# First projection weight tile and first two modulation tiles loaded whole, and every operation placed anew, in one layer of a hybrid RG-LRU and sparse-attention block

## The chip, the cores and the metric

The kernel runs on one core of one Trainium2 chip. The time is the device time of one execution in microseconds (us); lower is better. A profile shows one execution, with its own time. Engines are named as the profile names them: PE (matrix products; PEld is its loading of the stationary operand), DVE, ACT, POOL, and SP, which here only issues transfers. A few transfers are issued by ACT.

## The reference

One layer over 512 tokens of width 1024, batch 1, all in float32. What the opening of the kernel computes is the modulation and the normalised, modulated input:

```
mod = jax.nn.silu(c) @ ada_w[l] + ada_b[l]
sh1, sc1, g1, sh2, sc2, g2 = jnp.split(mod, 6, axis=-1)
h = modulate(rms_norm(x, pre_norm_mix[l]), sh1, sc1)      # h * (1 + sc1) + sh1
y = hybrid_mixer(h, w_in[l], ...)                         # z = h @ w_in, two head groups, @ w_out
x = x + (1.0 + g1) * rms_norm(y, post_norm_mix[l])
h = modulate(rms_norm(x, pre_norm_mlp[l]), sh2, sc2)
y = jnp.square(jax.nn.relu(h @ w_ff1[l])) @ w_ff2[l]
x = x + (1.0 + g2) * rms_norm(y, post_norm_mlp[l])
```

The mixer projects h, feeds one half of the columns to a gated linear recurrence with a causal convolution, and the others to an attention of three branches (compressed, selected and windowed keys), normalises both halves and projects them back. The last part is an MLP of width 4096 with a squared ReLU.

## The kernel before, in words

Float32 products are made of three float32r products: each operand is split into a rounded part (`hi`) and the rest (`lo`), and hi*hi, hi*lo and lo*hi are summed in PSUM. So for each weight tile an engine writes `hi` from the raw tile, another writes `lo = raw - hi`, and PE then has three products for each block.

**Opening.** Four x tiles of 128 x 1024 (`r_1` and `r_2` in the profile, two in each) are loaded by SP; each is normalised with a sum of squares (written to `att` as waste) and a power on POOL. The conditioning vector comes in two small transfers issued by ACT: `in_ccol` (128 x 8), of which `sil` is computed, and `in_vecs` (128 x 136), the gains and biases. From `sil` and the identity matrix `ident`, PE makes `silb`, silu(c) in a row, the same in every partition: four products for each half of it (`tp_104`, `tp_105`), which an engine then copies out. `ident`, `tab` and `ctab` (the last two are masks for the attention) are made on DVE.

**The wave.** The first projection takes 768 columns of h in eight steps j, one for each 128 input features. For each j two modulation tiles (`p`, 128 x 1024, from `in_ada_a`) are multiplied by `silb` and summed along the row on DVE (`ada_sums`): that gives 128 shifts and 128 scales, `sa`. PE transposes the four x blocks into `tp`; ACT writes h = tp * scale + shift, once rounded (`h_136`, `h_137`, ... are j = 0, 1, ...) and once exact (`pt`); DVE writes the rest (`h_144`, `h_145`, ...). Weight tile `raw_a` is split into `hi_a` and `lo_a`. Then come 18 products of 512 columns for each j: six PSUM tiles (two each of `f`, `s`, `pv`) by three products. Names of j = 0: tiles p_158 (shift) and p_159 (scale), sa_166, raw_a_160. Of j = 1: p_161, p_162, sa_176, raw_a_163. Of j = 2: p_164, p_165, sa_184.

Before the first product, 18 products of ones with ones (`s<-ones`) run on PE; nothing reads their result.

**What sets the order.** Each operation is recorded (`Clocks.put`, `flush`) and then issued in an order written out by hand: `PLAN` is a string of two characters for each operation, which are its place among all of them. `PLACE` is a string for each part of the program with one letter for each operation that more than one engine can do: a (ACT), d (DVE) or p (POOL). On each engine the instructions run in that order; semaphores keep the dependences. SP's and ACT's transfers are places in the same order. A place number says nothing about a time: an operation waits until its engine has reached it and its inputs are there.

In j = 0 the kernel loads the first two `p` tiles in halves of 512 columns and sums each half by itself, the second sum starting from the first one's result; and it loads `raw_a_160` in three pieces of 256 columns. All other tiles are loaded whole. `hi_a` and `lo_a` of j = 0 are made in pieces of 256 columns.

**After the wave.** The rest of the projections, the recurrence, the attention (scores `s`, probabilities `p`, transposed `pt`, weighted values `pv`), the output projection, and the MLP follow, in which blocks of products are merged to save some of them (`first_pair`, `up_pair`). PE has work of this kind until shortly before the end, and the output rows are normalised and stored.

Of the kernel before, what the change touches and what calls it, by code (L numbers as in the profile page):

```python
# [11 lines left out]
ALU = mybir.AluOpType  # L12
PSUM = bass.MemoryType.PSUM

P = 128
S = 512
# [1918 lines left out]
```

## Time and profile before

| | |
|---|---|
| median of 3 runs | 588.01 us |
| lowest and highest | 586.90, 588.99 us |
| the profiled execution's own time | 588.5 us |
| its span, first to last instruction | 586.7 us |
| PE, DVE, ACT, POOL busy | 572.7 (98%), 550.1 (94%), 416.5 (71%), 227.2 (39%) us |
| transfers | 89.12 MB, 192 issued by SP |

The execution that was profiled took 1.8 us more than its span, and 0.5 us more than the median of the runs. In a row of the timeline the first two numbers are the start and the length in us, `x16` counts merged instructions, and the bracket has the idle time of the engine before it and what ended that. A product in float32 shows two instructions for each one in the program's order.

### The profile page before, as it was taken

Reading aid. Unit: us, or ns where it says so; the run is one execution under the profiler, and the core shown is the slowest. Engines: PE = TensorE matmul, PEld = TensorE weight load, DVE = VectorE, ACT = ScalarE, POOL = GpSimd, SP = SyncE. Lnnn points to the kernel's source line nnn. Section 1 sums busy time; section 2 is a strip of 40 time slices with the busy share of each in tenths; the row PEclk is TensorE's granted clock in tenths of the full one; section 3 lists DMA queues with packets and bytes.
Section 4 is the critical chain, followed back from the end, with each engine's and each line's share of the span. In section 5 each row is a group of like instructions: output and inputs, shape, how many; then the busy total and the mean of one; then the engine's idle time right before and its main releaser. Section 6 shows DMA issues by size and latency. Waiting matters only on the chain.

```text
span 586.7 us, 9981 instructions
## 1 busy us (share of the span) xinstructions
PE 572.7 (98%) x3410; PEld 499.5 (85%) x3410; DVE 550.1 (94%) x1143; ACT 416.5 (71%) x849; POOL 227.2 (39%) x212
## 2 busy tenths in 40 slices
PE   6999999999999999999999999999999999999995
PEld 5688889878888898899999999998778888788884
DVE  5999999999999999999999999999999999998877
ACT  6658877999999999788747666574757676555314
POOL 4203323656847288651234242532101400114453
PEclk9999999999999999999999999999999999999999
DMA  8989895142242410022342423337343444344303
GB/s 314 417 314 344 295 396 220 59 142 73 94 177 91 151 65 1 19 91 73 109 147 106 139 77 108 110 120 273 129 154 121 157 140 151 122 144 155 132 1 144
DMA packets 27875, 89.12 MB, mean 152 GB/s; under 512 B 3360, under 2 KB 4272, under 8 KB 27824
## 3 DMA queue, kind: packets, MB, share of 16 engines
q1 hardware_dynamic: 27392, 88.27, 42.4%
q8 instruction: 27, 0.44, 0.3%
q10 hardware_dynamic: 432, 0.20, 0.1%
q14 instruction: 24, 0.20, 0.1%
HBM read 86.36 MB, written 2.11 MB: 151 GB/s over the span
## 4 chain that ended last, share of the span: by engine, by line
PE 86%; DVE 7%; issue 1%; ACT 1%; DMA 1%; POOL 0%; DVEq 0%; POOLq 0%
PE f L343 27%; PE pv L343 21%; PE s L343 20%; PE tp L343 14%; PE tp L346 4%; DVE r L387 2%; DVE p L387 2%; DMA ar<-in_ada_r 1%; DVE fT L387 0%; DVE lo_D L387 0%; ACT junk L353 0%; POOL stat L387 0%; DVE K L387 0%; DVE lo_q L387 0%; DVE h L387 0%
## 5 line engine op out<-in xcount | busy, mean ns | idle before, releaser
L387 POOL TENSOR_SCALAR p<-p,den 128x32 f32<-128x32 f32 (+4 forms) x48 | 46.3, 977 | 17.9 <-DVE den L387 10.4
L353 ACT ACTIVATE p<-p,mx 128x32 f32<-128x32 f32 (+4 forms) x96 | 45.2, 474 | 3.9 <-DVE mx L387 3.7
L343 PE MATMUL f<-hi_o,h 128*128 128x512 f32 x128 | 44.5, 406 | 0.0
L353 ACT ACTIVATE fT<-fT 128x512 f32<-128x512 f32 x50 | 29.5, 620 | 9.8 <-DVE fT L387 9.7
L346 PE MATMUL tp<-ident,p 128*128 128x128 f32 x192 | 36.3, 274 | 0.0
L343 PE MATMUL pv<-pt,V 128*128 128x256 f32 x160 | 36.3, 303 | 0.0
L343 PE MATMUL s<-K,Q 128*128 128x288 f32 (+4 forms) x128 | 36.1, 333 | 0.0
L387 DVE TENSOR_TENSOR pt<-tp,pt 128x512 fp32r<-128x512 f32 (+1 forms) x56 | 34.0, 607 | 2.0 <-ACT pt L353 0.5
L353 ACT ACTIVATE hi_B<-raw_A 128x512 fp32r<-128x512 f32 x32 | 20.1, 629 | 19.8 <-DVE raw_A L387 11.6
L387 DVE CUSTOM_DVE_ANT_0 p<-p,silb 128x1024 f32<-128x1024 f32 (+1 forms) x24 | 28.9, 1217 | 0.7 <-DMA p<-in_ada_a 0.7
L343 PEld LDWEIGHTS pv<-pt,V 128*128 128x128 f32 x160 | 26.7, 190 | 3.0 <-DVE pt L387 0.9
L346 PEld LDWEIGHTS tp<-ident,p 128*128 128x128 f32 x192 | 24.4, 141 | 4.8 <-issue 1.3
L343 PEld LDWEIGHTS f<-hi_o,h 128*128 128x128 f32 x128 | 23.5, 188 | 3.6 <-issue 0.3
L353 ACT ACTIVATE pt<-tp 128x512 fp32r<-128x512 f32 (+1 forms) x46 | 24.3, 534 | 3.0 <-PE pv L343 1.6
L353 ACT ACTIVATE junk<-r 128x1024 bf16<-128x1024 f32 (+2 forms) x17 | 13.7, 807 | 16.7 <-DVE r L387 16.2
L343 PEld LDWEIGHTS s<-K,Q 128*128 128x128 f32 x128 | 22.5, 188 | 3.3 <-PE f L343 0.4
L353 ACT ACTIVATE hi_D<-raw_d 128x1024 fp32r<-128x1024 f32 x14 | 14.8, 1060 | 14.1 <-DVE raw_d L387 9.7
L343 PE MATMUL f<-lo_o,h 128*128 128x512 f32 x64 | 24.8, 397 | 0.0
L353 ACT ACTIVATE hi_e<-raw_e 128x1024 fp32r<-128x1024 f32 x13 | 13.7, 1057 | 13.9 <-PE pv L343 5.0
L343 PE MATMUL f<-third,hi_B 128*128 128x256 f32 x96 | 23.4, 284 | 0.0
L387 POOL TENSOR_TENSOR fl<-fS,fh 128x256 fp32r<-128x256 f32 x3 | 6.5, 2176 | 42.6 <-ACT fh L353 42.6
L343 PE MATMUL tp<-r,hi_B 128*128 128x256 f32 x96 | 22.9, 283 | 0.0
(441 smaller groups left out, 2349.8 us busy)
## 6 DMA issues: line engine op xcount, KB each, us to landing
p<-in_ada_t SPq DMA_DIRECT2D x16, 512.0 KB, 7.0
ar<-in_ada_r SPq DMA_DIRECT2D x16, 512.0 KB, 4.3
p<-in_ada_a SPq DMA_DIRECT2D x14, 512.0 KB, 7.2
raw_d<-in_wd SPq DMA_DIRECT2D x14, 512.0 KB, 3.2
raw_e<-in_wd SPq DMA_DIRECT2D x14, 512.0 KB, 3.3
raw_A<-in_wf SPq DMA_DIRECT2D x12, 512.0 KB, 3.2
raw_B<-in_wf SPq DMA_DIRECT2D x12, 512.0 KB, 3.3
r<-in_x SPq DMA_DIRECT2D x8, 512.0 KB, 5.7
```

The source lines that it names most:

```text
L343: lambda: self.nc.tensor.matmul(out, lhs, rhs, start=start, stop=stop))
L346: self.issue("pe", 0.109, [out], [src], lambda: self.nc.tensor.transpose(out, src, ident))
L353: return "act", cost, lambda: self.nc.scalar.activation(out, src, func, scale=scale, bias=bias, **kw), func
L387: return eng, cost, lambda: fn(out, *args, **kw), None
```

## The change

Three things are changed, and the tables. (1) `raw_a` of j = 0 is loaded whole instead of in three pieces. (2) The first two `p` tiles are loaded whole instead of in halves. (3) Their sums are made over the whole tile: two DVE sums of 1024 columns in place of four of 512. (4) `PLAN` and `PLACE` are replaced: the order of nearly all operations changes on each engine, and some change their engine.

```diff
 PLAN = (
-    '#0#1#5#=#6#>#8#:#9#2#7#a#H#I#J#K#[#L#M#N#O#Z#$#&###(#)#+#*#,#/#%#.#o#-#p$C#n#G#P#Q#R#S#z#{#|#}#~$#$$'
...
 )
-PLACE = {'': 'da',
+PLACE = {'': 'dd',
-         'XN': 'aaaaaaaaaaaapadapaa',
+         'XN': 'aapaaaaaaadaaaadaa',
...
     for j in range(KD):
-        cuts = [slice(256 * n, 256 * n + 256) for n in range(3)] if j == 0 else [slice(0, 768)]
-        W.add(f"a{j}", 768, [(lambda r, sl=sl: r[:, sl], inp["wa"][j][:, sl]) for sl in cuts])
+        W.add(f"a{j}", 768, [(lambda r: r[:, :768], inp["wa"][j])])
...
             k = len(ada) - 1
-            for sl in [half(0), half(1)] if k < 2 else [slice(0, 1024)]:
-                load(ada[-1][:, sl], inp["ada_a"][k][:, sl])
+            load(ada[-1], inp["ada_a"][k])
...
             for e, first in enumerate((b, 0.0)):
                 w = ada[2 * j + e]
-                if j == 0:
-                    part = scol()
-                    dve("tensor_tensor_reduce", w[:, half(0)], w[:, half(0)], silb[:, half(0)], 1.0, first, ALU.mult,
-                        ALU.add, part)
-                    dve("tensor_tensor_reduce", w[:, half(1)], w[:, half(1)], silb[:, half(1)], 1.0, part, ALU.mult,
-                        ALU.add, sa[:, e:e + 1])
-                    continue
                 dve("tensor_tensor_reduce", w, w, silb, 1.0, first, ALU.mult, ALU.add, sa[:, e:e + 1])
```

The rows of the order below name an operation, what it writes and reads, and its size. ACT at the program's start, before and then changed:

```order
L451 DMA vecs<-in_ccol 128x8
L451 DMA vecs<-in_vecs 128x136
L353 ACT_TABLE_LOAD
L353 ACTIVATE sil<-vecs 128x8
L353 ACTIVATE att_129,stat<-r_2_87 128x512 x2
```

```order
L451 DMA vecs<-in_vecs 128x136
L451 DMA vecs<-in_ccol 128x8
L353 ACT_TABLE_LOAD
L353 ACTIVATE sil<-vecs 128x8
L353 ACTIVATE att_129,stat<-r_2_87 128x512 x2
```

The two small transfers have changed places on ACT's queue: the one that `sil` needs is now issued second.

DVE at the program's start, before:

```order
L387 TENSOR_SCALAR ident<-p_89 128x128
L387 TENSOR_SCALAR tab<-p_89 128x512
L387 SCALAR_TENSOR_TENSOR sil<-sil,vecs 128x8
L387 TENSOR_SCALAR ctab<-p_97 128x128
L387 TENSOR_SCALAR cmask<-p_97 128x1
L387 TENSOR_TENSOR ctab<-ctab,p_97 128x128
```

and changed:

```order
L387 TENSOR_SCALAR ctab<-p_97 128x128
L387 SCALAR_TENSOR_TENSOR sil<-sil,vecs 128x8
L387 TENSOR_SCALAR tab<-p_89 128x512
L387 TENSOR_TENSOR ctab<-ctab,p_97 128x128
L387 TENSOR_TENSOR tab<-tab,p_89 128x512
L387 TENSOR_SCALAR ident<-p_89 128x128
```

`ident` has moved from the first row of DVE to the sixth, behind `sil` and three operations on the masks.

The same engine from the second half of `silb` to the sum of p_161, in the change (before, ACT copied that half out, and four sums of 512 columns stood in place of the first two):

```order
L387 TENSOR_SCALAR silb<-tp_105 128x512
L387 TENSOR_TENSOR sp<-sp 128x4
L387 ISA p_158,sa_166<-p_158,silb,vecs 128x1024
L387 ISA sa_166 128x1
L387 ISA p_159,sa_166<-p_159,silb 128x1024
L387 ISA sa_166 128x1
L387 SCALAR_TENSOR_TENSOR sa_166<-sa_166,ab_102,vecs 128x1
L387 TENSOR_SCALAR sp<-sp 128x4
L387 TENSOR_SCALAR r_2_87<-r_2_87,stat 128x128
L387 TENSOR_TENSOR lo_a_174<-raw_a_160,hi_a_173 128x256 x2
L387 ISA p_162,sa_176<-p_162,silb 128x1024
L387 ISA sa_176 128x1
```

```order
L387 TENSOR_TENSOR lo_a_174<-raw_a_160,hi_a_173 128x256
L387 SCALAR_TENSOR_TENSOR sa_176<-sa_176,ab_102,vecs 128x1
L387 TENSOR_TENSOR h_144<-pt_170,h_136 128x512
L387 ISA p_165,sa_184<-p_165,silb 128x1024
L387 ISA sa_184 128x1
L387 ISA p_161,sa_176<-p_161,silb,vecs 128x1024
```

What stands in these rows between the first sum and the sum of p_161 is what DVE does before j = 1 has its shifts: five whole sums, three pieces of `lo_a`, the rest of h, and four small operations.

On PE the products of `ones` were, before, one ahead of the products for `silb`, and 17 behind them (14 in a row, then one and two among the transposes). In the change:

```order
L343 MATMUL s_155<-ones 128x128 x4
L343 MATMUL tp_104<-ident,sil 128x128 x4
L343 MATMUL tp_105<-ident,sil 128x128
L343 MATMUL s_155<-ones 128x128
L343 MATMUL tp_105<-ident,sil 128x128 x3
L343 MATMUL s_155<-ones 128x128 x4
L346 MATMUL tp_179<-ident,r_1_86 128x128
L343 MATMUL s_155<-ones 128x128 x5
```

Four of the 18 now run ahead of `silb`'s, one between them.

On SP's queue the four x tiles now come first, then p_158, p_159, raw_a_160, p_162 and raw_a_163 whole; before, the first 256 columns of raw_a_160 were the third transfer, the halves of p_158 and p_159 came in turn behind the x tiles, and the other two pieces of raw_a_160 behind p_162. SP issues 188 transfers instead of 192.

Elsewhere the kinds of work on each engine stay nearly as they were. The largest shifts in the attention are multiplications of probabilities by `den`: DVE has one more of 128x384 and two more of 128x32, ACT two fewer of 128x384, one fewer of 128x256 and one fewer of 128x32, POOL one more of 128x384, one more of 128x256 and one fewer of 128x32. PE has the same number of instructions. Its last rows are the same nine products of 256 columns into `s`, and the operations behind them are the same ones.

More of the change, by code (lines that the diff above doesn't have):

```diff
@@ L166 @@
[L166 to L174 removed]
+    '#.#-#7#h#4#6#2#5#;#/#3#c#@#A#B#C#d#D#F#G#H#i#$#%###&#(#)#*#q#+#,#r#p#<#=#>#?#E#I#w#x#y#{#|#}#~$#$($)'
@@ new lines @@
+    '$*$.#J#Q#R#[#V$5#L#S#U#]#Z$3#1#0#O#P#`#W$4#Y#X#^#_#o#v$[#k#l#m$C$B$$$%$&$,$1$0$2$<$A$D#t$8#u$:#s$7$E'
+    '$L$V$S$i$T$N$M$n$m$k$U$O$W$p$o$l$j$Y$>$9$;$F$G#z$+$-$/$H$I$J$6$?%-$t$q$s$x$r$v$w%%$u$y${%4$z%=$~%#%C'
+    '%7$@$=$K%.%,$P$Q$R$X$]$^$b$Z$`%3%;%>%6%$%L%8%<%?%A%5%N%9%B%I%D%@%O%:$e$a$d%0%/$|$}%&%(%+%*%[$_$f%p%T'
+    '%z%E%Q%P%W%V%|%F%U%S%u%x%}&#%w%v&%$g$h%]%2%1%G%H%K%M%a%b%g%)%_%s%~&$&,%y%{&J&2&(&4&-&5&K&N&+&H&.&E&L'
+    '%`%Z%^%J%R%X%Y%d%e%k%c%i%r&W&1&I&D&F&P&Y&3&Q&M&R&S&Z&G&U&O&V&T%j%f%h&&&*&/&0&9&:&?&;&@()&k&`&a&d&X&q'
@@ new lines @@
+    '&o&h&b&e&^&s&p&j&c&l&_&t%o%l%n&)&6&7&8&<&>&B&=&C(f&u&y&f&m(C&w&v(@&g&n(F&x&z(A&i&r(G(B#M(%(5(0(8&|&~'
+    '&{&}($(#(u(v,^%q(r(m)X(~(*(1(2(:(4(7(q(y(;(6(|({)S)c)T)g(s+K(n(l+`*W*|-k)U)`+_*1&A(&(.%t(-(((/(h(z(k'
+    ')d)i*3(j*U)l*Z)m*[)j*_*q+#*r+**t+,*v+a*x,/1&/Z0M5R#T+c(<#N)()Q&](,(=(>(?(i&[(+(g(3(9#8#9#K#a#b#e#f#g'
+    '#j#n$c%m(D(E(H)#(o(w)$)e*0*V*Y*^,e-@/4(I(J(K/5#:/7/;/b(L(M(O(S(X(Y(Z(](^(`(a(b(c(d(e**(t(})&*]++.;/W'
+    '(N(P(Q(R(T(U(V(W(p(x)%([(_))),)1)2)3)4)R)W)h)5);)<)>)?)@)A)B)P)f)k)D)F)G)H)I)J)K)M)V)b*-*p)])_)a)*)+'
@@ new lines @@
+    ')-).)/)0)6)7)8)9):)=)C)E)L)N)O)Y)Z)[)^)p)q)r*,*&*.*s)n)o)s)t)u)v)w)x*)*/*u)y)z){)|)})~*#*4*+*X*w*6*8'
+    '*9*:*;*<*=*?*~+-,_*5*>*A*B*C*D*E*H*I*K*P*Q*R*S*T*a*b*c*d*e*f*g*m*o*}*z+$+)+O+d,]*@*F*G*J*L*M*N*O*`+Q'
+    '+b,`*j*k*y*h*i*l*$*%*{*(,m*2+/+0+3+7+M+L+W+Z+.+1+2+4+5+6+:+;+<+=+>+?+@+A+B+C+D+E+F+G+H+P,),+,a+R+S+T'
+    '+U+e+f+g+h+i+j+k+l+m+n+o+p+q+r+t+u+v+w+x+y,&-h.m0T-6-r.=.u+z,0,1,.-5-v/=,2,3,4-4-u-w/X,6,8,<,@,A,B,C'
+    ',D,E,F,G,H,I,J,K,L,M,N,h,k,Z,c*7*n+&+N+(,(+%,#+I+J+],[+V+}+^,%,g,i,l,s,t,q,w,p,r,5,7,:,;,=,>,?,O,Q,S'
@@ new lines @@
+    ',T,U,n,o,x,y,z,{,|,~-&-/-0-1-<-C->-D-,-2-3-G-H-I-J-K-L+8+9+X,$+[+~+Y,Y-M-N-O+{+|,,,V,*,X,-,W,v-7-E-e'
+    '-d-g-;-:-9-S-T-U-V-W-X-]-^-`-a-b-c-l-x-n/V-(-)-+---8-A-*-.-=-q-Y.*.-.2.3.>.?.@.A.f/Y0X,P,R,f,u,j-i.B'
+    '.C.E+s,9,d-j.F.G.H.I.K.P/]/e0U.Q.R.V.[.].b/0/</11%/c024#/6-P-_.+.,...0.5.s.t-}.$.(.).4.:.%.1.7.X-#-%'
+    '-?-f-F-m,}-$-B-o-y-z.k.o-|.8.6-{.D.L.N.O.S.c/H/[/^-Q-R-p.h-s.l-Z-[-t.e.^._.`.a.j.v.J.~/%/*/2/U-~.#.9'
+    '.d.W.i.&./.<.g.n/3/P/Q/S/L/O/R.{/&/A/D/(/>/M/d/h/i/n/o.T.U.q/..p/T.Y.Z.r///q/{0D0L0R/~0$0%0&0/01/m/t'
@@ L184 @@
-         'AV': 'aaaaaadaadadaaaaaaaaadaadadaaadaaaaaaaaaddaaaaaaaaadaaaa',
+         'AS': 'paaapaapppappppappaapppppaapdpdpappdppaaaappppapppaaapapdpddpapdadppaddpdpapappapapapapappppdapa'
+          'appppappdddaappa',
+         'AV': 'aaaaaaaaadadaaaaaaaaaaaadadaaadadaadaaaaddaaaaaaaaadaaaa',
          'VW': 'ppppdpppdpppddd',
-         'FA': 'dddpppppdddd',
-         'AD': 'a',
+         'FA': 'pddppppppddd',
+         'AD': 'd',
          'RS': 'ppdpdaddadda',
-         'TH': 'aappdadddaddadddaadpdaddaaddaapddaddaddaddaddddd',
@@ L198 @@
+         'G2': 'd',
+         'DN': 'adappapdadaddaddadaddadpadaddaddadaddaddapaddaddadaddaddadaddaddadaddadpadaddaddadaddaddadaddadd'
+          'adaddaddadaddappadadadapadadadapadadadadadddadadadadadapapadadadapapadadddaddpapdpdddddpd'}
 class Clocks:
```

219 lines of the change are left out of this document (97 added, 122 removed).

## The prediction

> **What bounds the kernel now.** I read first how busy each engine is by stretch, then the waits of PE, then the opening instruction by instruction. The rows of the first view are start:end, length, and the busy time (with instruction count) of PE, PEld, DVE, ACT, POOL; then granted clock, DMA share, GB/s.
>
> ```profile
> 15.05:21.20 6.15, 5.55 (x23) 3.58 (x23) 5.72 (x14) 3.74 (x6) 3.43 (x3) 1.00 1.03 418
> 21.20:52.00 30.80, 30.80 (x146) 25.12 (x146) 30.70 (x53) 20.95 (x30) 2.03 (x2) 1.00 0.92 359
> 52.00:570.00 518.00, 516.77 (x3132) 453.86 (x3131) 492.48 (x1025) 375.53 (x775) 209.05 (x184) 1.00 0.38 132
> 570.00:587.00 17.00, 9.90 (x55) 8.44 (x53) 12.12 (x24) 6.39 (x17) 5.06 (x6) 0.94 0.34 124
> ```
>
> From 21.20 on, where the products of j = 1 begin, PE is busy for 30.80 us of 30.80, then for 516.77 of 518.00. So 548.8 us behind the opening are PE's own work, with 518.00 - 516.77 = 1.23 us of idle time. The change takes no product away: an instruction count for PE that stays equal means that only the time before 21.2, those 1.23 us, and the last 17 us can be gained. The longest waits in the middle are these (total, count, longest, in us):
>
> ```profile
> PE pv L343 <- DVE lo_f L387: 0.4, 1, 0.4
> PE f L343 <- ACT r L353: 0.3, 1, 0.3
> PE s L343 <- DVE lo_D L387: 0.2, 1, 0.2
> PE pv L343 <- POOL h2l L387: 0.2, 1, 0.2
> ```
>
> Each is a single wait, so there is no repeated one that a new order removes at a stroke. In the last 17 us the order's last PE rows and what stands behind them are the same, so I take nothing there. What remains is the opening, where PE still waits for others. In timeline rows the first number is the start, the second the length.
>
> ```profile
> 1.59 0.80 PE L343 MATMUL s<-ones 128*128 128x128 f32 x2 [1.59 <-POOL ones L711]
> ...
> 4.23 0.21 ACT L353 ACTIVATE sil<-vecs 128x8 f32<-128x8 f32 x1 [1.29 <-DMA vecs<-in_ccol]
> 4.47 0.17 DVE L387 SCALAR_TENSOR_TENSOR sil<-sil,vecs 128x8 f32<-128x8 f32 x1 [2.39 <-ACT sil L353]
> 4.69 3.60 PE L343 MATMUL tp<-ident,sil 128*128 128x128 f32 x16 [2.30 <-DVE sil L387]
> 5.95 0.17 DVE L387 TENSOR_SCALAR sp<-vecs 128x4 f32<-128x4 f32 x1 [0.84 <-DMA vecs<-in_vecs]
> 8.12 3.29 PE L343 MATMUL s<-ones 128*128 128x128 f32 x28
> ```
>
> This is the start of the chain that leads to the first product: the small transfer `in_ccol`, `sil` on ACT and on DVE, then the eight products for `silb` (two passes each, so x16). They take 3.60 / 16 = 0.225 us a pass; the products of ones behind them take 3.29 / 28 = 0.117 us. PE's fast passes came 8.12 - 4.69 = 3.4 us after it had begun to work steadily.
>
> **The change part by part.**
>
> **1. The two small transfers change places.** In the trace the first of the two, `in_ccol`, releases ACT at 4.23; the second, `in_vecs`, releases DVE at 5.95. I take the order on the queue to be what sets these times, so that `in_ccol`, now second, can be used from 5.95. Bounds: 4.23, if the place in the queue does not matter, and 6.15, for which I allow an eighth of the 1.72 between the two. ACT's `sil` then starts at 5.95 and DVE's 0.24 later (4.47 - 4.23), at 6.19.
>
> **2. `ident` is made sixth.**
>
> ```profile
> 1.42 0.24 DVE L387 TENSOR_SCALAR ident<-p 128x128 f32<-128x128 f32 x1 [1.42 <-POOL p L705]
> 1.56 0.52 DVE L387 TENSOR_SCALAR tab<-p 128x512 f32<-128x512 f32 x1
> 4.81 0.29 DVE L387 TENSOR_TENSOR ctab<-ctab,p 128x128 f32<-128x128 f32 x1
> 6.37 0.68 DVE L387 TENSOR_TENSOR tab<-tab,p 128x512 f32<-128x512 f32 x1
> ```
>
> Before, `ident` was ready at 1.66, 3 us before PE needed it at 4.69. Now DVE stands at `sil` until 6.19 and then does `sil` 0.17, `tab` 0.52, `ctab` 0.29, `tab` 0.68 and `ident` 0.24: 1.90, less about 0.08 for each of four overlaps with the next one (on DVE an instruction of 1.22 us is followed 1.15 later, rows below) = 1.58. `ident` is ready at 7.77, and PE starts on `silb` at about 7.85, not 4.69. This is the largest single step of the change: 3.16 us.
>
> **3. PE's passes for `silb`.** Eight products and one of ones among them are 18 passes. At 0.225 until 3.4 us after the start (11.25) that is 15 passes, and 3 more at 0.117: done at 11.6. Bounds: all fast, 7.85 + 18 x 0.117 = 9.95; all slow, 11.9. What speaks for fast is that four products of ones now run earlier; what speaks against it is that PE then stands still until 7.85, and that before it was slow at 4.69, after two passes of ones and a pause. I take 11.6.
>
> [...]
>
> **4. Both halves of `silb` on DVE, whole tiles, whole sums.**
>
> ```profile
> 7.04 0.68 DVE L387 TENSOR_SCALAR silb<-tp 128x512 f32<-128x512 f32 x1
> 9.95 0.75 DVE L387 CUSTOM_DVE_ANT_0 p<-p,silb,vecs 128x512 f32<-128x512 f32 x1 [0.15 <-DMA p<-in_ada_a]
> 11.42 0.70 DVE L387 CUSTOM_DVE_ANT_0 p<-p,silb 128x512 f32<-128x512 f32 x1 [0.71 <-DMA p<-in_ada_a]
> 12.17 0.79 DVE L387 CUSTOM_DVE_ANT_0 p<-p,silb,stat 128x512 f32<-128x512 f32 x1
> 12.88 0.74 DVE L387 CUSTOM_DVE_ANT_0 p<-p,silb,stat 128x512 f32<-128x512 f32 x1
> 13.96 1.22 DVE L387 CUSTOM_DVE_ANT_0 p<-p,silb 128x1024 f32<-128x1024 f32 x1
> 15.11 0.61 DVE L387 TENSOR_TENSOR lo_a<-raw_a,hi_a 128x256 fp32r<-128x256 f32 x1
> 18.24 0.69 DVE L387 TENSOR_TENSOR h<-pt,h 128x512 fp32r<-128x512 f32 x1
> 18.85 1.28 DVE L387 CUSTOM_DVE_ANT_0 p<-p,silb,vecs 128x1024 f32<-128x1024 f32 x1
> 20.05 0.35 DVE L387 SCALAR_TENSOR_TENSOR sa<-sa,ab,vecs 128x1 f32<-128x1 f32 x2
> 20.36 0.78 ACT L353 ACTIVATE h<-tp,sa 128x512 fp32r<-128x512 f32 x1 [1.40 <-DVE sa L387]
> 21.20 0.50 PE L343 MATMUL s<-h,hi_a 128*128 128x512 f32 x1
> ```
>
> Four half sums are 0.75 + 0.70 + 0.79 + 0.74 = 2.98 us; two whole ones are 1.22 + 1.28 = 2.50. That saves about 0.5 us of DVE. But before, the first two were done while the second tiles were still coming (DVE idle 0.15 and 0.71, for DMA); now no sum starts before the whole `silb` stands. The second half's copy, 0.68 on DVE, ends at 11.6 + 0.68 = 12.3: p_158's sum starts there, where DVE before had two of the four halves behind it.
>
> From there the front's rows of DVE give: two sums with `vecs` at 1.20 (18.85 to 20.05) and three at 1.15 (13.96 to 15.11) = 5.85; three pieces of `lo_a` at 0.6 = 1.8; the rest of h 0.61 (18.24 to 18.85); two rows of `sa` 0.27; one of `sp` and one of `r` 0.3. Sum 8.83: p_161's sum ends at 12.3 + 8.83 = 21.13, where p_161's place was taken before by a sum that ended at 20.05.
>
> **5. To the first product of j = 1.** Before: sums end 20.05, two rows of `sa`, ACT's h at 20.36, the product at 21.20, 0.84 later. In the change the shift's sum comes last and needs no further row; h starts 0.05 after it: 21.13 + 0.05 + 0.84 = 22.0. That is **+0.8** against 21.20.
>
> ```profile
> 13.98 1.02 ACT L353 ACTIVATE h<-tp,sa 128x256 fp32r<-128x256 f32 x2 [1.32 <-DVE sp L387]
> 14.36 2.37 POOL L387 TENSOR_SCALAR hi_a<-raw_a 128x256 fp32r<-128x256 f32 x2 [1.69 <-DMA raw_a<-in_wa]
> 15.05 0.73 PE L343 MATMUL s<-h,hi_a 128*128 128x512 f32 x2 [1.34 <-ACT h L353]
> ```
>
> Do the products of j = 0 end later than that? Their scale and shift stand at 12.3 + 2.4 + 0.1 = 14.8, r at 15.1, PE's transposes 0.4, ACT's h 1.02: first product 16.6 against 15.05. Eighteen at 0.227 (products follow one another so in steady rows) are 4.1, and with the 0.45 that two transposes cost the end is 21.15, before 22.0. So PE will stand idle for about 0.8 us there, and what sets the start of j = 1 is DVE's sums.
>
> **6. `raw_a_160` whole.** POOL's `hi_a` now waits until 14.36 for pieces of it. In the new order SP issues 3.54 MB up to its end (four x tiles, two `p` tiles, itself), before 4.06 up to its last piece, p_162 among them.
>
> ```profile
> 10.00:15.00 5.00, 3.55 (x27) 2.71 (x25) 4.25 (x12) 3.21 (x9) 3.12 (x5) 1.00 1.03 397
> ```
>
> A `p` or x tile is 128 x 1024 x 4 bytes, 0.52 MB; at this stretch's 397 GB/s that is 1.3 us sooner. It buys nothing: `lo_a` stands behind DVE's first two sums, which end near 14.8. If it came late all the same, the products of j = 0 would slip, and they have 22.0 - 21.15 = 0.85 of room before j = 1 feels that. For p_158: its first half was there at 9.95, with 2.49 MB issued up to its end (four x tiles, 256 columns of `raw_a`, the half); the whole has 2.62. The 0.13 more are 0.33 us, so it is there at 10.3, before 12.3: covered by the late `silb`, and the wait from 10.3 on if that cover is gone.
>
> Opening: **+0.8**. Its low bound: `in_ccol` at 4.23 and all passes fast; then the sum waits for its tile, 10.3 instead of 12.3, j = 1 starts at 20.0, -1.2. Its high bound, slow passes to the end and `in_ccol` at 6.15: 0.3 + 0.2 more, +1.3.
>
> **7. The middle.** All places are new, so waits of 0.2 to 0.4 as in the list above may go or come. At most 1.23 goes. I take 0, with -1.2 to +1.2 for single waits. **The last 17 us:** 0.
>
> The profiled execution takes 588.5: 588.5 + 0.8 = 589.3. It lay 0.5 above the median of 588.01; the comparison is with medians, so the forecast is 588.01 + 0.8 = **588.8**.
>
> **The rivals.**
>
> B, faster: **the opening is paced by transfers and not by `silb`.** If the second place on ACT's queue costs nothing, or PE stays fast, the low bound holds, -1.2, and the new places take some of the 1.23 of idle time, say 0.8: 588.0 - 1.2 - 0.8 = 586.0. For it: DVE waits for DMA before both first sums now (0.15 and 0.71), and SP has four transfers fewer. Against it: `ident` behind four DVE operations is in the order, whatever the transfers do. With `in_ccol` at 4.23 `ident` would be there at 4.47 + 1.58 = 6.05, PE would start at 6.1 and be done by 15 slow and 3 fast passes at 9.85, and the sum would start at 10.5, 0.2 behind its tile: most of the gain would stand whatever the clock does. So B hangs on `in_ccol` more than on PE's passes.
>
> C, slower: **DVE becomes the bound in the attention.**
>
> ```profile
> 100.00:150.00 50.00, 50.00 (x280) 41.44 (x279) 48.67 (x145) 48.07 (x125) 31.21 (x28) 1.00 0.30 103
> 150.00:200.00 50.00, 50.00 (x287) 42.32 (x286) 47.58 (x145) 48.84 (x131) 31.45 (x31) 1.00 0.32 117
> ```
>
> and, grouped over this part (count, total in us, mean in ns, idle before):
>
> ```profile
> L387 DVE TENSOR_SCALAR p<-p,den 128x32 f32<-128x32 f32 x4 | 1.0, 257 | 0.0
> ...
> L387 DVE TENSOR_SCALAR p<-p,den 128x384 f32<-128x384 f32 x1 | 0.4, 411 | 0.0
> ```
>
> DVE is busy 48.67 and 47.58 of 50 us there, with 3.75 us free in 100. The change moves 0.411 + 2 x 0.257 = 0.93 us of multiplications onto it. Of DVE's remaining 2.8 us some fall where no input is ready; if that is 2 of the 2.8, PE, which never waits there now, waits for `p` or its transposes as long: with the opening +0.8, 588.0 + 2.8 = 590.8. It decides when DVE's share there passes 98.5% and PE shows idle time between 100 and 200. Against it: ACT and POOL take other work over, and PE has 0.00 idle there, so there is some depth of buffered work.
>
> That the change does less than it says, D: the new opening makes no difference, since PE has 0.60 us of idle time between 15.05 and 21.20 (5.55 of 6.15 busy) that may take a part of the delay, and fewer waits in the middle the rest; time unchanged, 588.0. It lies in A's range and I count it there.
>
> **How the numbers follow.** A, 588.8: 0.52. Its own range is 587.6 to 589.8, the 1.2 us of the middle below and 1.0 above (waits, or the opening's high bound). B, 586.0: 0.20. C, 590.8: 0.28. The range, 586.2 to 591.2, reaches to the centre of B and past that of C; the outer half of B and the outer third of C are about 0.2. A measurement of this kernel can tell about 0.3% from no change, 586.25 to 589.77: A and D lie within, B below, C above. So faster 0.20, same 0.52, slower 0.28.
>
> **What would show it.** ACT's `sil` at 5.95 with its wait for `in_ccol` (step 1); DVE's `ident` near 7.5 and PE's first `tp<-ident,sil` near 7.85 (2); its passes 0.225 us apart for 3.4 us (3); the 1024-wide sum of p_158 at 12.3 (4); the first product of j = 1 at 22.0 with PE idle before it (5). Between 52 and 570, PE's idle time stays near 1.2 (7); more than 2.5 and DVE near its limit in 100 to 200 would be C. The forecast is wrong if `sil` starts near 4.2, if the products of j = 1 start before 21.2, or if PE's idle time in the middle changes by more than 1.2 us.

## The result: 0.85% slower, against a forecast of no change

The changed kernel takes 593.15 us (median of six runs, 592.63 to 593.27), the kernel before 588.00 (six runs). The ratio is 1.0085, with a 95% interval of 1.0072 to 1.0098: about 5.0 us are lost, where the forecast was 0.8 and its range ended at 591.2. In the profiled executions the span grew from 586.7 to 591.3, by 4.6 us.

The stretches of the changed kernel, with the columns that the prediction named (start:end, length, busy time of PE, PEld, DVE, ACT, POOL, clock, DMA share, GB/s):

```profile
0.00:15.05 15.05, 8.99 (x48) 8.69 (x49) 9.31 (x24) 8.54 (x22) 9.28 (x21) 1.00 0.88 341
15.05:21.20 6.15, 5.19 (x31) 4.08 (x30) 6.11 (x15) 4.51 (x7) 0.00 (x0) 1.00 1.01 411
21.20:52.00 30.80, 30.80 (x147) 25.09 (x146) 30.74 (x55) 20.68 (x30) 0.98 (x1) 1.00 0.96 350
52.00:570.00 518.00, 513.12 (x3116) 450.45 (x3115) 493.37 (x1015) 373.88 (x770) 209.26 (x190) 1.00 0.38 132
570.00:591.30 21.30, 14.51 (x75) 12.20 (x74) 15.55 (x30) 7.87 (x21) 4.45 (x5) 0.89 0.27 99
```

The first stretch of the kernel before, which the prediction did not show:

```profile
0.00:15.05 15.05, 9.66 (x60) 8.52 (x60) 9.13 (x31) 9.87 (x24) 7.66 (x20) 1.00 0.88 317
```

PE does the same work, so its idle time is the account. To 21.2 it was idle for 5.39 + 0.60 = 5.99 us before, and for 6.06 + 0.96 = 7.02 now: 1.03 more. From 52 to 570 it was idle for 1.23 us before and for 4.88 now: **3.65 more**. Behind 570, up to the end of the spans, it was idle for 16.7 - 9.90 = 6.80 before and 21.30 - 14.51 = 6.79 now. The three differences add up to 4.67, within 0.1 of the span's 4.6. So the opening did about what was forecast, and the loss lies in the middle, which the prediction had costed at nothing. The waits of PE there (total, count, longest):

```profile
PE pv L343 <- POOL fl L387: 1.4, 1, 1.4
PE s L343 <- DVE mx L387: 1.4, 1, 1.4
PE pv L343 <- ACT pt L353: 0.7, 1, 0.7
PE tp L343 <- POOL lo_e L387: 0.7, 1, 0.7
```

Four single waits, 4.2 us together, beside three of 0.2, are there now; before, the longest were four of 0.2 to 0.4.

**What is late at each of them.** `fl` and `lo_e` are the exact remainders of split operands, `mx` the maxima of the attention scores. POOL's rows, then what DVE does at the same time:

```profile
497.57 4.38 POOL L387 TENSOR_TENSOR fl<-fS,fh 128x256 fp32r<-128x256 f32 x1 [76.73 <-ACT fh L353]
...
501.90 0.73 POOL L387 TENSOR_TENSOR fl<-fS,fh 128x256 fp32r<-128x256 f32 x1
...
525.54 4.88 POOL L387 TENSOR_TENSOR lo_e<-fT,hi_e 128x512 fp32r<-128x512 f32 x1 [8.20 <-ACT hi_e L353]
```

```profile
497.07 1.28 DVE L387 TENSOR_TENSOR fl<-fT,fh 128x512 fp32r<-128x512 f32 x2
498.27 0.41 DVE L387 TENSOR_TENSOR fS<-fT,fS 128x256 f32<-128x256 f32 x1
498.61 1.28 DVE L387 TENSOR_TENSOR t<-raw_e,t 128x512 f32<-128x512 f32 x2
499.81 0.41 DVE L387 TENSOR_TENSOR fl<-fS,fh 128x256 fp32r<-128x256 f32 x1
500.15 1.21 DVE L387 TENSOR_TENSOR lo_e<-raw_e,hi_e 128x1024 fp32r<-128x1024 f32 x1
```

The same operation of 256 columns takes POOL 0.73 us at 501.90 and 4.38 us at 497.57. All through the long one DVE runs operations with two operands from SBUF, one behind the other without a pause, until 501.36; POOL ends 0.59 later. That is nearly the 0.73 us of the whole operation; so, read from these times, POOL had not been working slowly: it had not been working. Before the change this `fl` was DVE's and took 0.42 us; it is one of those that the new table of engines gave to POOL. The `lo_e` at 525.54, DVE's before as well, is the same case.

At 88 us the two engines have changed parts (the modulation sum `p<-p,silb` also reads two operands from SBUF, and so does `lo_v`):

```profile
87.82 2.50 POOL L387 TENSOR_TENSOR lo_v<-raw_v,hi_v 128x840 fp32r<-128x840 f32 x1
88.38 3.02 DVE L387 CUSTOM_DVE_ANT_0 p<-p,silb 128x1024 f32<-128x1024 f32 x1
```

The sum, 1.24 us at 86.55, took 3.02. It ended at 91.40, 1.08 us after POOL's end at 90.32; so, by these times, it stood until POOL had ended. The maxima are queued behind it on DVE, and PE's next scores behind the maxima.

The wait for `pt` at 155 is of another kind. POOL stands for a sum that ACT's `p` releases late, and the multiplications by `den` are queued behind it:

```profile
151.77 0.20 POOL L387 TENSOR_TENSOR den<-sm,eg 128x6 f32<-128x6 f32 x1 [3.85 <-ACT p L353]
```

In these rows one engine stands while the other works. Which one began first does not settle it: at 88 us POOL, 0.56 us ahead, kept the sum waiting, but at 497.57 POOL began and still stood behind DVE operations that began from 497.67 on. Nor is POOL always kept out so long. In the same kernel it came in behind a single DVE operation, with no pause on DVE:

```profile
514.36 0.68 DVE L387 TENSOR_TENSOR lo_e<-fT,hi_e 128x512 fp32r<-128x512 f32 x1
514.96 1.79 DVE L387 TENSOR_TENSOR fT<-raw_e,fT 128x512 f32<-128x512 f32 x1
...
514.66 1.54 POOL L387 TENSOR_TENSOR lo_e<-fT,hi_e 128x512 fp32r<-128x512 f32 x1 [8.16 <-ACT hi_e L353]
```

Here DVE's second operation took 1.79 us instead of the 0.68 of the same one at 528.59, and ended 0.55 after POOL (516.75 and 516.20): by these times POOL went between the two. At 88 us it did so too: a DVE operation on `r` ran until 88.46, and POOL's `lo_v` ended 1.86 us after it, ahead of the sum, as in experiment 2 below it ended 1.86 after the sum. So beside a dense row on DVE, POOL may stand for one operation or for the whole row; what decides it, no run here shows.

### The profile page after: what moved, and what is told of

Its sections match the earlier page's. It is cut to its first block, busy times and chain, and to the rows that moved or that the text cites. A ratio compares the mean times of both kernels' runs of the same rounds, so it can differ in the third digit from the quotient of the medians.

```text
span 591.3 us, 9962 instructions
## 1 busy us (share of the span) xinstructions
PE 572.6 (97%) x3410; PEld 500.5 (85%) x3410; DVE 555.1 (94%) x1136; ACT 415.5 (70%) x848; POOL 224.0 (38%) x216
## 4 chain that ended last, share of the span: by engine, by line
PE 81%; DVE 9%; issue 5%; ACT 2%; POOL 2%; DMA 1%; ACTq 0%; DVEq 0%; POOLq 0%
PE f L343 26%; PE pv L343 19%; PE s L343 18%; PE tp L343 13%; PE tp L346 4%; DVE r L387 4%; DVE p L387 3%; DMA vecs<-in_ccol 1%; POOL lo_e L387 1%; POOL fl L387 1%; ACT junk L353 1%; ACT p L353 1%; DVE pt L387 0%; POOL stat L387 0%; ACT pt L353 0%
## 5 line engine op out<-in xcount | busy, mean ns | idle before, releaser
L387 POOL TENSOR_SCALAR p<-p,den 128x32 f32<-128x32 f32 (+4 forms) x49 | 45.1, 932 | 11.5 <-DVE den L387 4.7
L387 POOL TENSOR_TENSOR fl<-fS,fh 128x256 fp32r<-128x256 f32 x5 | 9.0, 1803 | 76.7 <-ACT fh L353 76.7
L343 PE MATMUL s<-K,Q 128*128 128x288 f32 (+4 forms) x128 | 34.5, 334 | 1.4 <-DVE mx L387 1.4
L387 DVE CUSTOM_DVE_ANT_0 p<-p,silb 128x1024 f32<-128x1024 f32 x24 | 31.1, 1315 | 0.1
L387 POOL TENSOR_TENSOR r<-r,vecs 128x248 f32<-128x248 f32 x7 | 7.2, 1067 | 43.1 <-ACT r L353 43.1
L387 DVE TENSOR_TENSOR lo_B<-raw_A,hi_B 128x512 fp32r<-128x512 f32 x30 | 22.1, 736 | 1.0 <-ACT hi_B L353 0.6
```

Source lines behind the costliest of these rows:

```text
L343: lambda: self.nc.tensor.matmul(out, lhs, rhs, start=start, stop=stop))
L387: return eng, cost, lambda: fn(out, *args, **kw), None
```

## The experiments

The theory: the 3.65 us of the middle are for the most part **collisions** of DVE and POOL, at places where the new order makes PE wait for the one that loses. The rivals: the late opening puts everything behind it out of step; or DVE is simply full (the prediction's rival C). All edits change only places or engines in the two tables, so the work is the same in all of them. Ratios are to the kernel before, measured on the same chip, with 95% intervals. The kernel before took 588.28 to 589.05 us (medians) beside the experiments, and the changed kernel was not run again beside them; so a difference of 1 or 2 us to the changed kernel is sure only where the spans show it too.

**1. `fl` back on DVE, at its place.**

```diff
-POOL TENSOR_TENSOR fl_701_1277<-fS13_903,fh_700_1276 128x256
+DVE  TENSOR_TENSOR fl_701_1277<-fS13_903,fh_700_1276 128x256
```

> The changed kernel with one operation back on DVE, at the same place of the order: the 256-column `fl` that POOL starts at 497.57 and ends at 501.94. Collision theory (POOL's two-input operation stands still while DVE runs two-input operations back to back beside it): on DVE it takes about 0.4 us, PE's wait of 1.4 us for it at 502 goes, and the time falls by 1.4 us to about 591.8. Theory that DVE is full (0.4 us more on DVE costs what it saves): PE waits about as long for another operation there, time 593 unchanged or later.

Measured 594.27, ratio 1.0093 (1.0078 to 1.0109): nothing gained. The wait for POOL's `fl` was gone, but DVE now stood for 1.51 us at that place, since ACT had not made `fh` yet, and everything behind it on DVE was later:

```profile
497.39 0.42 DVE L387 TENSOR_TENSOR fl<-fS,fh 128x256 fp32r<-128x256 f32 x1 [1.51 <-ACT fh L353]
```

So this run told nothing between the theories; it showed that a place that suits one engine's queue need not suit another's.

**2. The sum ahead of POOL.** One DVE operation that stood between two sums goes behind the maxima.

```diff
 DVE  ISA p_78_250,a2_233<-p_78_250,silb_103 128x1024
-DVE  SCALAR_TENSOR_TENSOR r8_84_271<-r8_82_254,vecs_85,r8_84_271 128x512
 DVE  ISA p_79_251,a2_233<-p_79_251,silb_103 128x1024
...
+DVE  SCALAR_TENSOR_TENSOR r8_84_271<-r8_82_254,vecs_85,r8_84_271 128x512
```

> The changed kernel with one DVE operation, the 128x512 `r<-r,vecs,r` that runs at 87.72, moved behind the block of seven maxima (`mx`), so that the modulation sum `p<-p,silb` which took 3.02 us from 88.38 is issued directly behind the sum before it, at 87.7, before POOL's `lo_v` (87.82 to 90.32) has begun. No operation is added, taken away or given to another engine. Collision theory (whoever of DVE and POOL begins first keeps the other waiting): the sum takes about 1.2 us, the maxima come some 2 us sooner, PE's wait of 1.4 us for `mx` goes, time about 591.8. Theory that the sum is slow for its own reason (its tile or its instruction): it takes 3 us again and the wait stays, time 593.1.

Measured 591.98, ratio 1.0053 (1.0041 to 1.0066), 1.9 us less than the changed kernel's 1.0085, and the span 2.0 us shorter (589.3); PE's wait for `mx` was gone.

```profile
87.48 1.22 DVE L387 CUSTOM_DVE_ANT_0 p<-p,silb 128x1024 f32<-128x1024 f32 x1
87.59 2.97 POOL L387 TENSOR_TENSOR lo_v<-raw_v,hi_v 128x840 fp32r<-128x840 f32 x1
```

With the same work and the same engines, the sum began 0.11 us ahead of POOL instead of 0.56 behind it: it took 1.22 us, and POOL waited: its `lo_v`, 2.97 us long, ended 1.86 after the sum. This is the collision theory's case.

**3 and 4. Opening and rest exchanged.** The new order to place 150 (about 25 us) and the old one behind it; and the old one to place 155 with the new one behind it. Both load whole tiles.

> The changed program (whole tiles, whole sums) with the new order and engines for the first 150 places (to about 25 us), and behind them the order and the engines of the kernel before. Theory that opening and middle are two separate losses: only the opening's stays, about 1.0 us (PE's idle time to 21.2 grew from 5.99 to 7.02), so 588.0 + 1.0 = 589.0, and PE's idle time from 52 to 570 near 1.2 us. Theory that the late opening puts the rest out of step: most of the loss is there, 592 or more, with PE idle 3 us or more from 52 to 570.

> The changed program (whole tiles, whole sums) with the old order and engines for the first 155 places (the two merged tiles loaded where their first halves stood, the sums where the second halves' stood, the whole raw_a of j = 0 as SP's third transfer), and behind them the new order and engines. Two separate losses: the opening's 1.0 us is won back, the stalls at 91, 155, 502 and 530 stay, time about 592. Late opening puts the rest out of step: the stalls go too, time 588 to 589.

Measured 588.79, ratio 1.0001 (0.9992 to 1.0010), and 593.71, ratio 1.0079 (1.0065 to 1.0093). With the old rest PE was idle for 1.16 us from 52 to 570, with the new rest for 5.54, whatever the opening was. That takes the late opening away as the cause of the middle's loss. The new opening with whole tiles cost less than was thought: its span was 0.7 us longer than before, and its time the same within 0.6 us. Experiment 4 missed its 592: its profile has a wait of 0.8 us near 313 (see 12) and, from 15 to 21.2 us, a granted clock of 0.72, so it does not tell what the old opening is worth.

**5. `fl` on DVE, two places later**, behind sums whose inputs are there.

```diff
 DVE  TENSOR_TENSOR fl_715_1301<-fT3_865,fh_714_1300 128x512
+DVE  TENSOR_TENSOR fl_701_1277<-fS13_903,fh_700_1276 128x256
...
-POOL TENSOR_TENSOR fl_701_1277<-fS13_903,fh_700_1276 128x256
```

> The changed kernel with the same `fl` of 256 columns on DVE as in the first experiment, but two places later, behind two sums of DVE's own whose inputs are there, so that DVE does not stand still for ACT's `fh` (it did for 1.51 us there). Collision theory: `fl` is ready at about 498.7 instead of 501.9, before PE needs it at 500.6; PE's 1.4 us of wait at 502 go and nothing takes their place, time lower than the changed kernel's by 1.4 us (ratio to the kernel before 1.0085 - 0.0024 = 1.006). Theory that DVE is full: the ratio stays at 1.0085.

Measured 592.75, ratio 1.0052 (1.0034 to 1.0069): by the ratios 1.9 us less than the changed kernel, in the profiles only 0.3 (span 591.0). PE was idle for nothing from 490 to 520, where DVE was busy for 29.86 of 30 us: it was nearly full there and could still take the 0.4 us more. This kernel also showed a wait of 0.8 us near 313 that the changed kernel had not; see 12.

**6. The reverse, in the kernel before**: the same `fl` from DVE to POOL, one letter.

```diff
-DVE  TENSOR_TENSOR fl_701_1277<-fS13_903,fh_700_1276 128x256
+POOL TENSOR_TENSOR fl_701_1277<-fS13_903,fh_700_1276 128x256
```

> The kernel before with one letter changed: the same `fl` of 256 columns (494.97 on DVE there, 0.42 us) goes to POOL at the same place of the order. Collision theory: POOL begins at 495.0, stands still until DVE's row of two-input operations ends (now 498.69, 0.3 earlier without this one) and ends near 499, about 4 us long; PE needs it at 497.34 and waits about 1.5 us; time 588.0 + 1.5, ratio 1.0025. Theory that POOL's own speed decides (about 0.75 us for such an operation with DVE idle): it ends at 495.8, PE waits for nothing, ratio 1.000.

A miss. Measured 588.27, ratio 0.9977 (0.9959 to 0.9996), no wait at 497:

```profile
494.81 0.68 DVE L387 TENSOR_TENSOR fl<-fT,fh 128x512 fp32r<-128x512 f32 x1
494.86 1.22 POOL L387 TENSOR_TENSOR fl<-fS,fh 128x256 fp32r<-128x256 f32 x1 [24.73 <-ACT fh L353]
495.77 1.39 DVE L387 TENSOR_TENSOR lo_e<-raw_e,hi_e 128x1024 fp32r<-128x1024 f32 x1 [0.28 <-ACT hi_e L353]
```

Taking `fl` off DVE made DVE reach its `lo_e` before ACT had made `hi_e`. It paused for 0.28 us, and POOL came in: it ended 0.59 after DVE's `fl` (495.49 to 496.08), and DVE's next took 1.39 instead of 1.23. So here POOL came in at a pause, and a row of which one operation is taken away may get a pause. It is not always needed: at 514.66 in the changed kernel POOL came in without one. That the ratio lies below 1 is not explained, as the waits of PE are those of the kernel before. That kernel took 589.05 beside this run, where it had 588.00 in the result, so the 588.27 need not be a gain.

**7. All four places.** The edits of 2 and 5, `lo_e` at 525 to DVE, and two multiplications by `den` on POOL, for the `pt` of the third wait, moved ahead of a sum that POOL was waiting for.

```diff
-POOL TENSOR_TENSOR lo_e61_1343<-fT8_870,hi_e61_1342 128x512
+DVE  TENSOR_TENSOR lo_e61_1343<-fT8_870,hi_e61_1342 128x512
...
+POOL TENSOR_SCALAR p_217_459<-p_217_459,den_220_462 128x32
+POOL TENSOR_SCALAR p_213_455<-p_213_455,den_220_462 128x32
 POOL TENSOR_TENSOR den_227_469<-sm_222_464,eg0_131 128x6
...
-POOL TENSOR_SCALAR p_217_459<-p_217_459,den_220_462 128x32
-POOL TENSOR_SCALAR p_213_455<-p_213_455,den_220_462 128x32
```

> The changed kernel with four edits of places at the four stalls: the DVE operation moved behind the maxima (88 us, as in the second experiment), `fl` on DVE two places later (498 us), one `lo_e` of 512 columns from POOL (525.54 to 530.42) to DVE between its neighbours, and two multiplications by `den` on POOL moved ahead of a sum of `den` for which POOL stood still until 151.77. The opening stays as changed. Collision theory: the stalls of 1.4, 1.4, 0.7 and 0.9 us go, 4.4 us together; the ratio falls from 1.0085 to about 1.001. Theory that the loss is spread over the whole order: it falls by less than half of that, to 1.005 or more.

Measured 590.39, ratio 1.0021 (1.0009 to 1.0033), span 587.6 instead of 591.3. The longest that are left of PE's waits:

```profile
PE pv L343 <- ACT pt L353: 0.3, 1, 0.3
PE pv L343 <- DVE pt L387: 0.3, 1, 0.3
```

Five operations out of 5462, moved, take back 3.8 of the 5.0 us, and 3.7 of the 4.6 us of span. The loss is not spread over the order, and the three collisions are shown to be most of it. PE was idle for 1.13 us from 52 to 570, less than before the change. The third wait, at 155, did not go: 0.71 us became the two of 0.33 and 0.29 above. The edit for it won next to nothing, and that POOL's queue is its cause stays an argument.

**8. `in_ccol` first again, in the changed kernel, and 9. second, in the kernel before.**

```diff
-ACT  DMA vecs_85<-in_vecs 128x136
 ACT  DMA vecs_85<-in_ccol 128x8
+ACT  DMA vecs_85<-in_vecs 128x136
```

> The changed kernel with the two small transfers on ACT's queue in the old order, `in_ccol` first; nothing else. By the prediction's first step `sil` on ACT starts at 4.2 again instead of 6.40, `ident` follows near 6.1, and the first product of j = 1 comes 1 to 2 us earlier than 22.4; the time falls by the PE idle time of the opening that this takes away, at most 1.0 us (ratio 1.0068 to 1.0085). If the place on the queue does not set these times, `sil` stays near 6.4.

> The kernel before with the two small transfers on ACT's queue changed over, `in_vecs` first; nothing else. By the prediction's first step `sil` on ACT starts at 5.95 to 6.4 instead of 4.23 and PE's first product with `ident` at 6.4 to 6.9 instead of 4.69; both halves of `silb` are copied 1.7 to 2.2 us later, so the first half sum starts at about 11.9 instead of 9.95 and the products of j = 1 about 1 us later; ratio 1.001 to 1.002. If the place on the queue does not set the landing, `sil` stays at 4.2 and the ratio at 1.000.

Measured, in the changed kernel: 592.27, ratio 1.0051 (1.0035 to 1.0067), 2.0 us less than 1.0085.

```profile
4.19 0.21 ACT L353 ACTIVATE sil<-vecs 128x8 f32<-128x8 f32 x1 [1.27 <-DMA vecs<-in_ccol]
5.93 2.50 PE L343 MATMUL tp<-ident,sil 128*128 128x128 f32 x10 [2.26 <-DVE ident L387]
...
20.21 0.19 PEld L343 LDWEIGHTS f<-h,hi_a 128*128 128x128 f32 x1 [0.20 <-ACT h L353]
```

In the kernel before: 590.73, ratio 1.0039 (1.0026 to 1.0052).

```profile
6.38 0.21 ACT L353 ACTIVATE sil<-vecs 128x8 f32<-128x8 f32 x1 [3.45 <-DMA vecs<-in_ccol]
```

The place on the queue alone moved `sil`: it starts at 4.23 and 4.19 with `in_ccol` first, at 6.38 and 6.40 with it second, in the kernel before and the changed one. With it put right the rest of the new opening is good: j = 1 starts at 20.2, 1.0 us ahead of the kernel before. In spans the change-over is worth 0.8 us in the changed kernel, where a wait of 0.8 us near 313 took a part of it back, and 1.1 in the kernel before; by the ratios the times moved by about twice that. In the changed kernel the medians themselves differ by 0.9 (593.15 and 592.27); in the kernel before the profiled execution, 589.61, was the second shortest of ten. What the rest is, is not known.

**10 and 11. Towards a faster kernel.** The four edits with `in_ccol` first; and these with `ident` directly behind `sil`.

```diff
 DVE  SCALAR_TENSOR_TENSOR sil<-sil,vecs 128x8
+DVE  TENSOR_SCALAR ident<-p_89 128x128
 DVE  TENSOR_SCALAR tab<-p_89 128x512
 DVE  TENSOR_TENSOR ctab<-ctab,p_97 128x128
 DVE  TENSOR_TENSOR tab<-tab,p_89 128x512
-DVE  TENSOR_SCALAR ident<-p_89 128x128
```

> The changed kernel with the four edits at the four stalls and `in_ccol` issued first again. Two losses that add: the four edits alone gave 1.0021, and `in_ccol` first brought the first product of j = 1 from 22.4 to 20.2, 1.0 us ahead of the kernel before (21.2); so the time goes to 1.0 us or somewhat more below that of the kernel before, ratio 0.997 to 0.999, span about 585.5. If the earlier opening only meets stalls further on (the kernel with `in_ccol` first alone had one of 0.8 us at 313 that the changed one had not), the ratio stays at 1.001 or more.

> As the kernel with four edits and `in_ccol` first, and `ident` made directly behind `sil` instead of behind three operations on the masks. By the prediction's second step PE starts on `silb` 1.2 us earlier (4.7 instead of 5.9). If `silb` sets the first sum it starts at 9.7 instead of 10.9, and the first product of j = 1 comes at 19.0 instead of 20.2, time lower by about 1 us (ratio 0.996). If the tile p_158, whole, lands at 10.3 as the prediction worked out, only 0.6 us of it are gained; if transfers pace the opening from there, nothing.

Measured 588.36, ratio 0.9998 (0.9989 to 1.0006), and 587.59, ratio 0.9991 (0.9981 to 1.0001). The first is as fast as the kernel before, with the wait near 313 in its profile. In the second, PE began on `silb` at 4.90 instead of 6.04, but the sum began at 10.25 and had waited for its tile:

```profile
10.25 1.28 DVE L387 CUSTOM_DVE_ANT_0 p<-p,silb,vecs 128x1024 f32<-128x1024 f32 x1 [0.78 <-DMA p<-in_ada_a]
```

10.3 is where the prediction put the landing of the whole tile. So the first sum now waits for its transfer, and j = 1 began no earlier: 20.08, against 19.87 in the first of the two.

The same opening was also put ahead of the old order:

> The changed program with the new order to place 150, in it `in_ccol` first and `ident` behind `sil`, and behind place 150 the order and engines of the kernel before. The new opening with the old rest had ratio 1.000 and PE idle for 6.7 us until 21.2; with `in_ccol` first that is 5.3 and with `ident` earlier 4.3 to 5.3. If the opening's gain stays to the end: ratio 0.996 to 0.998. If it is lost to waits further on: 1.000.

Measured 588.07, ratio 1.0000 (0.9988 to 1.0011), with executions from 587.29 to 591.10. PE was idle for 4.24 us to 21.2, the least of all, but the profiled execution, the longest of the twelve, shows two waits further on that no other kernel had:

```profile
PE s L343 <- ACT pt L353: 2.2, 1, 2.2
PE s L343 <- ACT h L353: 1.2, 1, 1.2
```

An opening that is early by 1 to 2 us was given back there. Where the shorter executions of it lose the gain is not known.

**12. The tie near 313.** In nine profiles with the new order at this place, five show no wait and four (4, 5, 8 and 10 above) one of 0.8 us of PE for `fT`. The changed kernel, with none (DVE, then POOL):

```profile
312.31 0.68 DVE L387 TENSOR_TENSOR lo_C<-raw_B,hi_C 128x512 fp32r<-128x512 f32 x1
312.32 1.83 POOL L387 TENSOR_TENSOR lo_B<-raw_A,hi_B 128x512 fp32r<-128x512 f32 x1
```

Experiment 5, with it:

```profile
312.34 1.83 DVE L387 TENSOR_TENSOR lo_C<-raw_B,hi_C 128x512 fp32r<-128x512 f32 x1
...
312.33 1.29 POOL L387 TENSOR_TENSOR lo_B<-raw_A,hi_B 128x512 fp32r<-128x512 f32 x1
```

Both start as POOL ends `raw_B` (312.36 and 312.38): DVE since it reads that, POOL since it is free. Their starts are 0.01 us apart. The one that began first took 0.68 us (DVE) or 1.29 (POOL), the other 1.83. In experiment 5 the other was DVE, and the `fT` behind it was 0.8 us late for PE. The last run took the tie away, on top of the kernel of experiment 11:

```diff
 DVE  TENSOR_TENSOR fT9_871<-f_561_946,fT9_871 128x256
-DVE  TENSOR_TENSOR lo_C51_956<-raw_B5_924,hi_C51_955 128x512
 DVE  TENSOR_TENSOR fT9_871<-pv_558_943,fT9_871 128x256
 DVE  TENSOR_TENSOR fT9_871<-pv_563_948,fT9_871 128x256
 DVE  TENSOR_TENSOR fT8_870<-tp_562_947,fT9_871 128x256
+DVE  TENSOR_TENSOR lo_C51_956<-raw_B5_924,hi_C51_955 128x512
```

> The kernel with the four edits, `in_ccol` first and `ident` behind `sil`, and one DVE operation more moved: the `lo_C` that starts at 312.31 in the changed kernel, within 0.01 us of POOL's `lo_B`, goes behind the three evictions `fT<-...` that follow it, which read only one operand from the same memory as POOL. Theory that the two exclude each other and the first one wins: POOL's `lo_B` always runs first (1.3 us), the evictions run beside it, `lo_C` follows at once, and PE's 0.8 us wait for `fT` near 313, which four of the nine profiles with this order show, cannot come any more; ratio a little below the 0.9991 of the kernel without this edit, 0.998 to 0.999. If the wait has another cause it shows again, or `lo_C` is late for PE now (first use 2 us after its old start) and PE waits for it instead: 0.999 or more.

Measured 587.90, ratio 0.9989 (0.9979 to 0.9999). The wait for `fT` did not come: POOL's `lo_B` took 1.29 us from 308.51, and beside it two of the evictions took 0.88 us together, as in the changed kernel. `lo_C` was late for PE instead, by less:

```profile
PE pv L343 <- DVE lo_C L387: 0.4, 1, 0.4
```

Its eleven executions lie between 587.67 and 588.19, those of experiment 11 between 586.26 and 588.70. So 0.4 us for certain stand in place of nothing or 0.8 us, and the times are closer together. That fits the tie; one profile without the wait for `fT` does not prove it alone. It is about 1% below the changed kernel; against the kernel before its gain of 0.1% is barely clear of its interval (its upper end is 0.9999). The lowest ratio of all is the 0.9977 of experiment 6, the kernel before with one letter changed, for which no cause was found; the reference was slower beside it.

## Why the prediction was wrong

**Steps 1 to 5, the opening: the chain was right and a little small; where PE stands idle was wrong.** `in_ccol` in second place, `ident` in sixth, slow passes, sum, first product of j = 1: each of the marks came late by a little. In the changed kernel:

```profile
6.40 0.21 ACT L353 ACTIVATE sil<-vecs 128x8 f32<-128x8 f32 x1 [3.47 <-DMA vecs<-in_ccol]
7.86 0.22 DVE L387 TENSOR_SCALAR ident<-p 128x128 f32<-128x128 f32 x1
8.14 2.50 PE L343 MATMUL tp<-ident,sil 128*128 128x128 f32 x10 [4.47 <-DVE ident L387]
10.86 1.49 PE L343 MATMUL tp<-ident,sil 128*128 128x128 f32 x6
13.11 1.49 DVE L387 CUSTOM_DVE_ANT_0 p<-p,silb,vecs 128x1024 f32<-128x1024 f32 x1
17.76 0.50 PE L343 MATMUL f<-h,hi_a 128*128 128x512 f32 x1 [0.67 <-ACT h L353]
21.60 0.78 ACT L353 ACTIVATE h<-tp,sa 128x512 fp32r<-128x512 f32 x1 [0.33 <-DVE sa L387]
22.27 0.66 PE L343 MATMUL f<-h,hi_a 128*128 128x512 f32 x2
```

`sil` at 6.40 (forecast 5.95, at most 6.15), PE at 8.14 (7.85), its 18 passes all slow for 4.2 us, 0.234 each, to their end at 12.35 (forecast 11.6, with the last three fast, 3.4 us after the start, a figure read from one start of the kernel before, which did not hold here), the sum at 13.11 (12.3), ACT's h at 21.60. The x2 in the last row holds the last product of j = 0 and the first of j = 1, whose weights are loaded at 22.43 (22.0). That is 1.2 us behind the kernel before, forecast 0.8; PE's idle time grew by 1.03. The choice between slow and fast passes was right. The four early products of ones did not help: PE stood still for 4.47 us behind them, and the passes were slow. What was wrong is step 5's 0.8 us of idle PE before j = 1, and with it the 0.85 of room in step 6. The first product of j = 0 came at 17.76 and not at 16.6, its products ended only when j = 1 was about to begin, and PE waited 0.2 us there; its new idle time lies ahead of 17.76.

**Step 6 and the last 17 us.** The whole tiles showed no cost: the kernel with the new opening and the old rest has the old time. No run has whole tiles as its only change. PE's idle time behind 570 is the same to 0.01 us.

**Step 7, the middle at 0 with 1.2 either way: this step failed.** It measured +3.65 us of idle PE. The prediction reasoned from what PE did not wait for in the kernel before: a few waits of 0.2 to 0.4, so a new order could add a few of that size. That is a list of the places where the old order had left something over, and no measure of what a new one can do. The prediction costed what was put **on DVE**, 0.93 us of multiplications, at DVE's own price. What was put **on POOL**, three `fl` and two `lo_e` of DVE's among it, it did not count, and there lay 2.1 of the 4.2 us of waits, beside a dense row on DVE: 0.42 us became 4.38. Another 1.4 us is the sum at 88, on DVE in both kernels, which the new order let come behind POOL's `lo_v`. The prediction had no term for the two engines keeping each other waiting. The kernel before shows the same thing at a place where it hurts nobody:

```profile
463.48 6.81 POOL L387 TENSOR_TENSOR fS<-fS,fT 128x256 f32<-128x256 f32 x1 [15.72 <-DVE fl L387]
```

An operation of this size, `fS`, took POOL 0.73 us at 500.18 and 6.81 here; DVE ran without a pause until 469.69, and POOL ended 0.60 later. Such rows were there to be read before the prediction was made.

**Rival C, slower, was the right side by another mechanism.** It put a loss of 2 us into 100 to 200, through a DVE above 98.5%. DVE was at 95 to 96% there, and PE idle for 0.12 and 0.93 us:

```profile
100.00:150.00 50.00, 49.88 (x283) 40.82 (x282) 47.97 (x142) 44.87 (x119) 33.57 (x30) 1.00 0.19 68
150.00:200.00 50.00, 49.07 (x279) 41.40 (x278) 47.80 (x147) 48.54 (x129) 29.65 (x30) 1.00 0.45 159
```

Experiments 5 and 7 show that DVE could take on the work. Its time, 590.8, was 2.3 us short. Rival B's opening (`in_ccol` at 4.2) is what experiment 8 made of the changed kernel: j = 1 at 20.2, where B had 20.0.

The mark that the prediction set, PE's idle time in the middle changing by more than 1.2 us, was the one that showed it wrong.

## What to carry to other kernels

When operations moved between DVE and POOL here, the price was not the operation's own time on the other engine. Look at what the first engine does at that moment: a two-operand operation on POOL beside an unbroken row of two-operand operations on DVE may stand until the row ends (`fl`, 4.38 us instead of 0.73), and a DVE operation that comes just behind POOL's may stand as well (the sum at 88 us, 3.02 instead of 1.24), so give POOL what is needed late, or what falls into a pause of DVE. A profile of few and short waits says that an order is good, not that the next one will be (waits of 0.2 to 0.4 us became 1.4); look in it for rows that took several times their usual length without harm (`fS`, 6.81 us instead of 0.73). That a small move at such a place does harm is the author's estimate.

## What the runs showed of the hardware that was not expected

POOL was kept out for whole rows of DVE instructions: its operations took 4.38, 4.88 and 6.81 us beside them, and 0.73, 1.29 and 0.73 for the same sizes at 501.90, 502.59 and, in the kernel before, 500.18. It came in when DVE paused for 0.28 us, and at 514.66 and 88 us also between two DVE instructions without a pause. What makes the difference is open.

Near 313, 0.01 us separated the starts of the two engines, and in the rows shown the one that began first took its usual time and the other 1.83 us; of nine profiled kernels with the same order at that place, five had no wait of PE for `fT` and four one of 0.8 us.

A DVE operation with one operand was long beside memory fills on POOL, which read nothing. At the start of the changed kernel:

```profile
1.72 1.81 POOL L429 MEMSET r<- 128x2048 f32 x1
1.81 2.70 DVE L387 TENSOR_SCALAR ctab<-p 128x128 f32<-128x128 f32 x1 [1.81 <-POOL p L720]
3.46 0.97 POOL L429 MEMSET K<- 64x1056 f32 x1
```

`ctab`, 0.22 us before the change, took 2.70 and ended at 4.51, 0.08 us after the second fill. That the fills held it is read from these times; no run varied it. It cost nothing here, since DVE's next operation waited for `sil` until 6.64.
